# Up-projections of a channel mixer as Strassen block products, with the down-projection interleaved in six parts

## The chip, the core and the metric

The kernel runs on one core of one Trainium2 chip. A core has five engines that work side by side, each through its own instructions in a fixed order: TensorE (PE in the profile, with its weight loads as PEld), VectorE (DVE), ScalarE (ACT), GpSimd (POOL) and SyncE (SP, which here only starts transfers). SBUF is the working memory with 128 partitions, PSUM holds what TensorE accumulates, in eight banks of 512 float32 columns. The metric is the device time of one execution in microseconds.

## The reference

One inference step of two layers over 640 tokens of width 1024: 512 tokens of a new stream, and 16 tokens of each of 8 running streams. Each layer is a mixer followed by a channel mixer on the same residual x. The first mixer is a gated one, the second is attention; neither is changed. The channel mixer is the part that matters:

```python
def _conv_ffn(x, prev, w_up, conv_w, w_down):
    z, st = _causal_dwconv(x @ w_up, conv_w, prev)   # width 3, along the tokens
    gate, up = jnp.split(z, 2, axis=-1)
    return (jax.nn.silu(gate) * up) @ w_down, st
# hp = _rmsnorm(xp, norm_ffn[layer]); D_MODEL = 1024, D_FF = 2816
```

w_up is 1024 x 5632 and w_down is 2816 x 1024. In blocks of 128 features, the up-projection gives 44 blocks (22 of the gate, 22 of the other branch), and the down-projection adds 22 blocks into 8.

## The kernel before

Activations lie with features on partitions and tokens along the free axis. A product keeps float32 accuracy by splitting each operand in two float32r parts, and multiplying three times: high by high, high by low, low by high. So one block of 128 outputs over one chunk of 128 inputs is three passes, each over two halves of 320 tokens: six matmuls of 128x128 weights with 320 moving columns (`mm`, L109). One up-block (8 chunks) is 48 of them.

Each block's weights (128 x 1024 float32) come in by one transfer, issued by SP (`weights`, L87). ScalarE makes the high part (whi, L88), VectorE subtracts for the low part (wlo, L89). Three buffers hold raw, whi and wlo each.

The channel mixer (`ffn`) walks j over 22 pairs of up-blocks: block j of the gate and block 22+j. For each pair TensorE does 96 matmuls. Then, for each of the two blocks, VectorE multiplies the sums by 1/rms of each token (rb) into a padded tile zp (L190, L191), GpSimd puts the running streams' state in (L183) and takes the new state out (L202), ScalarE does the first tap of the convolution (L196) and VectorE the other two (L198). ScalarE applies silu to the gate (L355), VectorE multiplies the two branches (L358, L359), and the product is split again (sh on ScalarE, L97, sl on VectorE, L98). The down-projection comes in four parts of 6, 6, 5 and 5 pairs: after the pairs of a part and one pair ahead, `project` goes through all 8 output blocks, and VectorE adds each into x (L209).

The norm's root is not needed ahead of the products. `prep` makes the operands hh and hl of x times the gain, adds the squares up on GpSimd (acc, L139), and `stats` and `spread` turn the sum into rb: a matmul against ones (L159), a power on GpSimd (L152), five diagonal tiles on VectorE (L170) and a second matmul (L174). The products are under way meanwhile.

The order within each engine is set ahead of time: the program is written in the order of the code, and a scheduling layer moves instructions of an engine past each other by its own estimates of when their inputs will be there. On the chip the engines take their instructions in that order, and wait for each other by semaphores.

## Time and profile before

| | us |
|---|---|
| median of 3 runs (1533.8 to 1535.37) | 1534.4 |
| profiled execution, first to last instruction | 1531.9 |
| PE busy | 1517.8 |
| DVE busy | 899.1 |
| ACT busy | 559.4 |
| POOL busy | 237.4 |
| DVE busy within 228 to 680 us, most of the first channel mixer (452 us) | 262.07 |
| POOL busy within 228 to 680 us | 73.04 |

The profile shows one execution. The share of busy time is taken over all stages together: in the channel mixers (about 215 to 680 us, and 1066 to 1529 us) PE hardly pauses, and DVE is busy somewhat over half of the time. A matmul's own duration (309 ns) is not its cost, since the next one starts before it ends; the cost is the distance between two starts. The median of the runs lies 2.5 us over the profiled span.

### The profile page before, as it was taken

How to read it: one execution, taken by the hardware profiler on the slowest of the kernel's cores; microseconds unless marked ns; L12 is line 12 of the kernel's file. 1: busy time of each engine (PE TensorE's matmuls, PEld its weight loads, DVE VectorE, ACT ScalarE, POOL GpSimd, SP SyncE). 2: the span in 40 equal slices, each digit the busy share in tenths (PEclk: the TensorE clock that was granted, in tenths of full speed). 3: DMA queues.
4: the chain of work that ended last, by engine and by line, in shares of the span. 5: the costliest groups of instructions: out<-in, count | busy, mean ns of one | idle time of the engine just before them, and what ended most of it. 6: DMA issues, size and time to landing. Idle time of an engine off the chain costs nothing.

```text
span 1531.9 us, 26648 instructions
## 1 busy us (share of the span) xinstructions
PE 1517.8 (99%) x11008; PEld 1473.5 (96%) x11008; DVE 899.1 (59%) x1541; ACT 559.4 (37%) x918; POOL 237.4 (15%) x281
## 2 busy tenths in 40 slices
PE   8999999999999999999999999999999999999999
PEld 6999999999999999999989888888999999999998
DVE  6545437644653655675676766768765466365463
ACT  5422334322322322345545454535432233133231
POOL 5000122201210201143111111003221021021010
PEclk9999999999999999999999999999999999999999
DMA  6222212222223222243544343523222222321313
GB/s 226 77 82 73 77 56 85 68 81 85 62 64 95 64 66 93 62 156 103 180 128 136 122 123 104 183 60 107 83 60 76 87 67 57 98 73 53 107 47 106
DMA packets 52296, 142.90 MB, mean 93 GB/s; under 512 B 6656, under 2 KB 13744, under 8 KB 52048
## 3 DMA queue, kind: packets, MB, share of 16 engines
q1 hardware_dynamic: 45424, 133.79, 28.6%
q10 hardware_dynamic: 6752, 7.41, 1.4%
q8 instruction: 87, 1.43, 0.4%
q14 instruction: 33, 0.27, 0.1%
HBM read 125.41 MB, written 11.54 MB: 89 GB/s over the span
## 4 chain that ended last, share of the span: by engine, by line
PE 96%; DVE 2%; issue 1%; ACT 1%; DMA 0%; POOL 0%; SPq 0%; DVEq 0%; ACTq 0%
PE mm L109 71%; PE pj L507 10%; PE pv L583 3%; PE po L109 2%; PE pt L576 1%; PE mm L239 1%; PE pt L662 1%; PE sc L569 1%; DVE hl L132 1%; PE sc L570 1%; DVE wlo L89 1%; PE scs L641 1%; PE pt L537 1%; PE pt L655 0%; PE scs L634 0%
## 5 line engine op out<-in xcount | busy, mean ns | idle before, releaser
L88 ACT CAST whi<-raw 128x1024 fp32r<-128x1024 f32 (+4 forms) x222 | 207.6, 937 | 494.6 <-PE mm L109 426.1
L109 PE MATMUL mm<-hl,whi 128*128 128x320 f32 x1664 | 379.4, 309 | 0.5 <-DVE hl L132 0.5
L109 PE MATMUL mm<-hh,whi 128*128 128x320 f32 x1664 | 379.8, 309 | 0.0
L109 PE MATMUL mm<-hh,wlo 128*128 128x320 f32 x1664 | 379.2, 309 | 0.0
L109 PEld LDWEIGHTS mm<-hl,whi 128*128 128x128 f32 x1664 | 278.2, 188 | 0.7 <-DVE hl L132 0.7
L109 PEld LDWEIGHTS mm<-hh,whi 128*128 128x128 f32 x1664 | 278.2, 188 | 0.1
L109 PEld LDWEIGHTS mm<-hh,wlo 128*128 128x128 f32 x1664 | 278.0, 188 | 0.0
L89 DVE TENSOR_TENSOR wlo<-raw,whi 128x1024 fp32r<-128x1024 f32 (+4 forms) x222 | 245.5, 1107 | 33.3 <-ACT whi L88 33.0
L109 PE MATMUL mm<-sh,wlo 128*128 128x320 f32 x866 | 197.2, 309 | 1.3 <-DVE wlo L89 1.3
L109 PE MATMUL mm<-sl,whi 128*128 128x320 f32 x866 | 197.2, 309 | 0.0
L109 PE MATMUL mm<-sh,whi 128*128 128x320 f32 x866 | 196.2, 309 | 0.0
L202 POOL COPY so<-zp 128x18 f32<-128x18 f32 x88 | 89.4, 1016 | 570.4 <-DVE zp L191 570.4
L190 DVE TENSOR_TENSOR zp<-mm,rb 128x512 f32<-128x512 f32 x88 | 60.9, 692 | 195.8 <-PE mm L109 195.8
L209 DVE TENSOR_TENSOR x<-mm,x 128x640 f32<-128x640 f32 x79 | 65.0, 823 | 185.6 <-PE mm L109 185.6
L198 DVE SCALAR_TENSOR_TENSOR t<-zp,cst,t 128x656 f32<-128x656 f32 x184 | 165.1, 900 | 10.3 <-ACT t L196 5.6
L109 PEld LDWEIGHTS mm<-sh,wlo 128*128 128x128 f32 x866 | 144.6, 188 | 1.6 <-DVE wlo L89 1.6
L109 PEld LDWEIGHTS mm<-sl,whi 128*128 128x128 f32 x866 | 144.8, 188 | 0.0
L109 PEld LDWEIGHTS mm<-sh,whi 128*128 128x128 f32 x866 | 144.4, 188 | 0.2 <-issue 0.2
L507 PE MATMUL pj<-wlo,hh 128*128 128x256 f32 x480 | 137.7, 287 | 0.7 <-DVE wlo L89 0.7
L507 PE MATMUL pj<-whi,hh 128*128 128x256 f32 x480 | 137.7, 287 | 0.0
L507 PE MATMUL pj<-whi,hl 128*128 128x256 f32 x480 | 137.5, 287 | 0.0
L507 PEld LDWEIGHTS pj<-wlo,hh 128*128 128x128 f32 x480 | 91.6, 191 | 2.8 <-issue 1.6
(188 smaller groups left out, 1691.3 us busy)
## 6 DMA issues: line engine op xcount, KB each, us to landing
raw<-w_up SPq DMA_DIRECT2D x88, 512.0 KB
raw<-w_dn SPq DMA_DIRECT2D x32, 384.0 KB
raw<-w_c SPq DMA_DIRECT2D x24, 512.0 KB
raw<-w_dn SPq DMA_DIRECT2D x32, 320.0 KB
raw<-w_ab SPq DMA_DIRECT2D x16, 512.0 KB
ck<-c_k SPq DMA_DIRECT2D x16, 512.0 KB
cv<-c_v SPq DMA_DIRECT2D x16, 512.0 KB
o_kv<-z ACTq DMA_DIRECT2D x8, 640.0 KB
```

The source lines that it names most:

```text
L88: nc.scalar.copy(out=hi[:, c], in_=raw[:, c])
L89: nc.vector.tensor_tensor(out=lo[:, c], in0=raw[:, c], in1=hi[:, c].bitcast(F32), op=ALU.subtract)
L109: nc.tensor.matmul(outs[h], lhsT=l, rhs=r[:, h * HT:(h + 1) * HT], start=start and k == 0, stop=stop and k == 2)
L132: nc.vector.scalar_tensor_tensor(out=lo, in0=x, scalar=gs, in1=hi.bitcast(F32), op0=ALU.mult, op1=ALU.subtract)
L190: nc.vector.tensor_tensor(out=op, in0=a[:, 0:TP], in1=b[:, 0:TP], op=ALU.mult)
L198: nc.vector.scalar_tensor_tensor(out=cv[:, 0:CW], in0=zp[:, i:i + CW], scalar=w[:, i:i + 1], in1=cv[:, 0:CW], op0=ALU.mult, op1=ALU.add)
L202: self.nc.gpsimd.tensor_copy(out=out.rearrange("p (s c) -> p s c", c=2), in_=zp[:, 496:ZW].rearrange("p (s c) -> p s c", c=18)[:, :, 16:18])
L209: self.nc.vector.tensor_tensor(out=x, in0=ps[:, C0:C0 + T], in1=x, op=ALU.add)
L239: nc.tensor.matmul(pvs[tb], lhsT=l[:, tb * P:(tb + 1) * P], rhs=r[:, (kc % 2) * 512:(kc % 2 + 1) * 512], start=kc == 0 and k == 0, stop=kc ...
L507: nc.tensor.matmul(out[tb], lhsT=l[:, tb * P:(tb + 1) * P], rhs=r[:, c:c + 256], start=kc == 0 and i == 0, stop=kc == 7 and i == 2)
L537: nc.tensor.transpose(t[:, tb * P:(tb + 1) * P], z[i][:, tb, pair * P:(pair + 1) * P], k.ident)
L583: nc.tensor.matmul(ov[64 * hh:64 * hh + 64, i * P:n], lhsT=z[2][:, j, (2 * pair + hh) * 64:(2 * pair + hh) * 64 + 64], rhs=u[:, j * P:(j + ...
```

## The change

The two up-blocks of a pair, times the two halves of the input features, times the two halves of the tokens, are a product of 2x2 blocks. It is now worked out with seven block products instead of eight (Strassen's scheme in Winograd's form). Each block product covers 128 outputs, 4 chunks of inputs (512 features: the even chunks or the odd ones) and 320 tokens, so 12 matmuls.

- `forms` replaces `prep` ahead of the channel mixers: for each two chunks of x it makes seven token operands, four of them sums or differences, and splits each in a high and a low part.
- `pair_weights` replaces two calls of `weights`: GpSimd makes four sums and differences of the pair's weights (s1 to s4, 512 columns each, L194 to L198), and ScalarE and VectorE split 3.5 tiles of 1024 columns (A, B, C and half a tile D) instead of 2 (L189, L190).
- `pair_blocks` does the seven products in three PSUM banks X, Z, Y. What is shared between outputs is copied out of a bank by ScalarE while the accumulation goes on (`snap`, four for each pair, L225), and added up on VectorE (L245, L253) and GpSimd (L252).
- `pad_halves` replaces `pad_evac`: three multiplications for each block instead of two (L262). The new state is taken out by ScalarE (L490) instead of GpSimd.
- The down-projection comes in six parts of 4, 4, 4, 4, 3 and 3 pairs, and the blocks of one part are spread among the pairs of the next. The first four pairs have none beside them. The last part follows behind the last pair.
- Pools: three zp tiles instead of four, five temporaries instead of nine in the channel mixers, PSUM as two tiles of two banks and four single banks. The rows of w_up are put into the order of KORD on the way in.

```diff
-PARTS = ((0, 6), (6, 12), (12, 17), (17, 22))
+PARTS = ((0, 4), (4, 8), (8, 12), (12, 16), (16, 19), (19, 22))
+KORD = (0, 2, 4, 6, 1, 3, 5, 7)
...
+    def forms(self, p, x, g, acc, fa, fb):
...
+        def plain(h, l, c, xs, gs):
+            nc.scalar.activation(out=h[:, c], in_=xs, func=AF.Copy, scale=gs)
+            nc.vector.scalar_tensor_tensor(out=l[:, c], in0=xs, scalar=gs, in1=h[:, c].bitcast(F32), op0=ALU.mult, op1=ALU.subtract)
+        plain(ah, al, A, x1[:, A], g1)
+        y1 = self.tmp()[:, 0:T]
+        nc.vector.tensor_scalar(out=y1, in0=x1, scalar1=g1, scalar2=None, op0=ALU.mult)
+        t1 = self.tmp()[:, 0:HT]
+        nc.vector.tensor_tensor(out=t1, in0=y1[:, B], in1=y1[:, A], op=ALU.subtract)
+        nc.scalar.copy(out=bh[:, B], in_=t1)
+        nc.vector.tensor_tensor(out=bl[:, B], in0=t1, in1=bh[:, B].bitcast(F32), op=ALU.subtract)
+        plain(ah, al, B, x2[:, A], g2)
+        plain(bh, bl, A, x2[:, B], g2)
...
+        stt(out=t2, in0=x2[:, B], scalar=g2, in1=t1, op0=ALU.mult, op1=ALU.subtract)
+        stt(out=t3, in0=x2[:, B], scalar=g2, in1=y1[:, B], op0=ALU.mult, op1=ALU.subtract)
+        stt(out=t4, in0=x2[:, A], scalar=g2, in1=t2, op0=ALU.mult, op1=ALU.subtract)
+        nc.scalar.copy(out=ch, in_=t)
+        nc.vector.tensor_tensor(out=cl, in0=t, in1=ch.bitcast(F32), op=ALU.subtract)
...
+    def pair_weights(self, wa, wb):
...
+        A = part(a, 1024, self.wp, w)
+        nc.gpsimd.tensor_tensor(out=s1, in0=b[:, 0:H], in1=b[:, H:2 * H], op=ALU.add)
+        nc.gpsimd.tensor_tensor(out=s2, in0=s1, in1=a[:, 0:H], op=ALU.subtract)
+        B = part(s[0], 1024, self.wp, w)
+        nc.gpsimd.tensor_tensor(out=s3, in0=a[:, 0:H], in1=b[:, 0:H], op=ALU.subtract)
+        nc.gpsimd.tensor_tensor(out=s4, in0=a[:, H:2 * H], in1=s2, op=ALU.subtract)
+        C = part(s[1], 1024, self.wp, w)
+        D = part(b[:, H:2 * H], H, self.fx, ("dhi", "dlo"))
...
+            self.product(X, w["x11"], f, "y1a", True)
+            self.product(Z, w["x12"], f, "y2a", True)
+            p1 = snap(X)
+            self.product(X, w["s2"], f, "t2", False)
+            Y = self.bank()
+            self.product(Y, w["s3"], f, "t3", True)
+        nc.vector.tensor_tensor(out=p1, in0=Z[:, 0:HT], in1=p1, op=ALU.add)
+        u2 = snap(X)
+        self.product(X, w["s1"], f, "t1", False)
+        p7 = snap(Y)
+        self.product(Y, w["x22"], f, "t4", False)
+        v = snap(X)
+        self.product(X, w["s4"], f, "y2b", False)
+        nc.gpsimd.tensor_tensor(out=v, in0=v, in1=p7, op=ALU.add)
+        nc.vector.tensor_tensor(out=u2, in0=Y[:, 0:HT], in1=u2, op=ALU.add)
+        return (p1, X[:, 0:HT]), (u2, v)
...
             for n, (a, b) in enumerate(PARTS):
+                acts, left = [], list(range(8))
                 for j in range(a, b):
-                    if j not in acts:
-                        acts[j] = up(j)
-                if n + 1 < len(PARTS):
-                    acts[b] = up(b)
+                    acts.append(up(j))
+                    if before is not None:
+                        m = -(-len(left) // (b - j))
+                        down(n - 1, before, [(ob,) for ob in left[:m]])
+                        left = left[m:]
+                before = acts
+            down(len(PARTS) - 1, before, [(0, 1)] + [(ob,) for ob in range(2, 8)])
```

How the change moves instructions is seen at three places. Numbers at the end of a name tell tiles apart.

The first place is PE where the first channel mixer begins. Before, the matmuls that turn the norm's sum around (L159, L174) stand among the up-products (mm<-hh, mm<-hl):

```order
L109 MATMUL mm_2009<-hh_1572,whi_2003 128x320 x2
L109 MATMUL mm_2009<-hl_1573,whi_2003 128x320 x2
L109 MATMUL mm_2009<-hh_1572,wlo_2004 128x320 x2
L109 MATMUL mm_2009<-hh_1578,whi_2003 128x320
L159 MATMUL aux_1964<-ones,acc_1571 128x1 x5
L109 MATMUL mm_2009<-hh_1578,whi_2003 128x320
L109 MATMUL mm_2009<-hl_1579,whi_2003 128x320 x2
```

Now (L302 and L317 are the same two steps, sh and sl the last block of the first mixer's projection, fa the new token operands):

```order
L110 MATMUL mm_1964<-sl_1455,whi_1959 128x320 x2
L110 MATMUL mm_1964<-sh_1454,wlo_1960 128x320 x2
L302 MATMUL u_2044<-ones,acc_1477 128x1 x5
L317 MATMUL u_2060<-t_2054,ones 128x128 x4
L317 MATMUL u_2061<-t_2054,ones 128x128
L215 MATMUL u_2102<-fa_1590,whi_2082 128x320
L215 MATMUL u_2102<-fa_1591,whi_2082 128x320
```

Both steps now stand behind the last projection block and ahead of the first up-product, with nothing between them; before, up-products stood ahead of them and between them. At the start of the second channel mixer it is the same.

The second place is DVE in the middle of a channel mixer. Before, one pair:

```order
L190 TENSOR_TENSOR zp_88<-mm_2544,rb_1973 128x512
L191 TENSOR_TENSOR zp_88<-mm_2544,rb_1973 128x8x16
L89 TENSOR_TENSOR wlo_2674<-raw_2672,whi_2673 128x1024
L198 SCALAR_TENSOR_TENSOR t_2646<-zp_88,cst,t_2646 128x656 x2
L190 TENSOR_TENSOR zp_90<-mm_2593,rb_1973 128x512
L191 TENSOR_TENSOR zp_90<-mm_2593,rb_1973 128x8x16
L89 TENSOR_TENSOR wlo_2802<-raw_2800,whi_2801 128x1024
L198 SCALAR_TENSOR_TENSOR t_2655<-zp_90,cst,t_2655 128x656 x2
L358 TENSOR_TENSOR t_2659<-t_2646,t_2655 128x512
L359 TENSOR_TENSOR t_2659<-t_2646,t_2655 128x128
L98 TENSOR_TENSOR sl_2663<-t_2659,sh_2662 128x640
```

Now, half of a pair with its two blocks of the down-projection (L190 are the subtractions for the weights of the next pair, L90 those for the down-projection; L341 are the taps that L198 were, L498 and L499 the product of the branches, L99 is its split):

```order
L190 TENSOR_TENSOR wlo_3337<-s_3323,whi_3336 128x1024
L341 SCALAR_TENSOR_TENSOR t_3243<-zp_89,cst,t_3243 128x656
L245 TENSOR_TENSOR sn_3370<-u_3345,sn_3370 128x320
L90 TENSOR_TENSOR wlo_3470<-raw_3468,whi_3469 128x512
L498 TENSOR_TENSOR t_3247<-t_3233,t_3243 128x512
L499 TENSOR_TENSOR t_3247<-t_3233,t_3243 128x128
L262 TENSOR_TENSOR zp_90<-sn_3370,rb_2053 128x320
L99 TENSOR_TENSOR sl_3251<-t_3247,sh_3250 128x640
L90 TENSOR_TENSOR wlo_3502<-raw_3500,whi_3501 128x512
L253 TENSOR_TENSOR sn_3398<-u_3384,sn_3398 128x320
L190 TENSOR_TENSOR dlo_3555<-raw_3533,dhi_3554 128x512
```

The other half holds five more L262, two additions into x (L352), the subtractions for A and B of the next pair and three more L341: 23 instructions for a pair, where 11 rows with 13 instructions stood before and the down-projection came apart.

The third place is POOL in the same stretch. Before, it moves small columns alone, two of each for a pair (three blocks are shown):

```order
L202 COPY so_1994<-zp_90 128x18
L183 COPY zp_90<-si_1993 128x8x2
L202 COPY so_1994<-zp_89 128x18
L183 COPY zp_89<-si_1993 128x8x2
L202 COPY so_1994<-zp_91 128x18
L183 COPY zp_91<-si_1993 128x8x2
```

Now, one pair:

```order
L194 TENSOR_TENSOR s_3536<-raw_3533 128x512
L197 TENSOR_TENSOR s_3537<-raw_3532,raw_3533 128x512
L252 TENSOR_TENSOR sn_3426<-sn_3426,sn_3412 128x320
L195 TENSOR_TENSOR s_3536<-s_3536,raw_3532 128x512
L198 TENSOR_TENSOR s_3537<-raw_3532,s_3536 128x512
L260 COPY zp_90<-si_2073 128x8x2
L260 COPY zp_88<-si_2073 128x8x2
```

Five additions and subtractions over whole rows of SBUF have come to POOL for each pair, and the copies of the new state have gone from it.

174 lines of the change are left out of this document (131 added, 43 removed).

## The prediction

> **What bounds the kernel now.** I read the busy table and the chain of waits on the page first, then the busy times of the stretch from 228 to 680 us, which is nearly all of the first channel mixer, then the chain in order of time around the places where the two channel mixers begin.
>
> ```profile
> span 1531.9 us, 26648 instructions
> PE 1517.8 (99%) x11008; PEld 1473.5 (96%) x11008; DVE 899.1 (59%) x1541; ACT 559.4 (37%) x918; POOL 237.4 (15%) x281
> PE 96%; DVE 2%; issue 1%; ACT 1%; DMA 0%; POOL 0%; SPq 0%; DVEq 0%; ACTq 0%
> ```
>
> ```profile
> 228.00:680.00 452.00, 452.00 (x3084) 452.00 (x3083) 262.07 (x356) 150.84 (x179) 73.04 (x90) 1.00 0.27 82
> 1043.40:1069.60 26.20, 24.45 (x167) 23.85 (x165) 26.07 (x24) 16.11 (x24) 13.34 (x7) 1.00 0.40 128
> ```
>
> ```profile
> 220.26 1.01 PE aux L159 x10
> 221.27 4.80 PE mm L109 x32
> 226.07 1.11 PE aux L174 x10
> 227.19 452.76 PE mm L109 x3087
> 1063.46 0.81 DVE x L209
> 1066.35 2.90 PE mm L109 x18
> 1069.26 1.01 PE aux L159 x10
> 1070.26 4.80 PE mm L109 x32
> 1075.06 1.11 PE aux L174 x10
> ```
>
> The second fence gives, after the length, the busy times of PE, PEld, DVE, ACT and POOL, then the granted clock. PE is never idle in the channel mixers, and one chain piece of 3087 matmuls lasts 452.76 us: 0.1467 us from one matmul to the next. DVE is busy 58% of that stretch, POOL 16%. There is one other bound: from 1043.4 to 1069.6 us DVE is busy 26.07 of 26.20 us. So fewer matmuls shorten the program as long as DVE, ACT and POOL keep up.
>
> **The matmuls.** A pair takes 84 instead of 96, of the same shape, each with its own weight load as before. 12 x 0.1467 = 1.76 us; 44 pairs give **-77.4 us** (the order has 3696 up-products in place of 4224). The down-projection keeps its count. A middle pair with its two blocks of 24 matmuls now asks for 132 x 0.1467 = 19.36 us, one of the first four pairs of a layer, with nothing beside it, for 12.32. Transfers carry the same bytes.
>
> **VectorE.** Its prices:
>
> ```profile
> L198 DVE SCALAR_TENSOR_TENSOR t<-zp,cst,t 128x656 f32<-128x656 f32 x184 | 165.1, 900 | 10.3 <-ACT t L196 5.6
> L209 DVE TENSOR_TENSOR x<-mm,x 128x640 f32<-128x640 f32 x79 | 65.0, 823 | 185.6 <-PE mm L109 185.6
> L190 DVE TENSOR_TENSOR zp<-mm,rb 128x512 f32<-128x512 f32 x88 | 60.9, 692 | 195.8 <-PE mm L109 195.8
> L191 DVE TENSOR_TENSOR zp<-mm,rb 128x128 f32<-128x128 f32 x88 | 24.8, 282 | 0.0
> L774 DVE TENSOR_TENSOR x<-po,x 128x320 f32<-128x320 f32 x16 | 7.4, 486 | 1.3 <-PE po L109 1.1
> ```
>
> ```profile
> 370.90 0.28 DVE L191 TENSOR_TENSOR zp<-mm,rb 128x128 f32<-128x128 f32 x1
> 371.10 1.22 DVE L89 TENSOR_TENSOR wlo<-raw,whi 128x1024 fp32r<-128x1024 f32 x1
> 372.23 1.83 DVE L198 SCALAR_TENSOR_TENSOR t<-zp,cst,t 128x656 f32<-128x656 f32 x2
> ```
>
> The last two rows show that an instruction starts 0.08 us before the one ahead of it ends, so 1.22 costs 1.14. A middle pair now has 23 of them: three weight subtractions of 1024 columns (3.66), three of 512 (2.07, at the 0.69 of L190), four taps (3.60), the branches' product (0.97) and its split (0.82, as L209), two sums of 320 columns (0.97), six pieces of zp (2.2: two of 320, two of 192 at about 0.35, two of 128), two additions into x (1.65). That is 15.9, less 22 x 0.08: **14.2 us of 19.36**. By itself this fits. A first pair has 11.5 us for 12.32.
>
> **GpSimd's new work on VectorE's port.** What one does to the other shows at the start of the program:
>
> ```profile
> 8.95 14.71 POOL L139 TENSOR_TENSOR acc<-acc,t 128x640 f32<-128x640 f32 x7 [7.88 <-ACT t L138]
> 9.63 5.88 DVE L132 SCALAR_TENSOR_TENSOR hl<-x,gv,hh 128x640 fp32r<-128x640 f32 x3 [0.46 <-ACT hh L131]
> 15.44 2.58 DVE L89 TENSOR_TENSOR wlo<-raw,whi 128x1024 fp32r<-128x1024 f32 x1
> 17.94 4.29 DVE L132 SCALAR_TENSOR_TENSOR hl<-x,gv,hh 128x640 fp32r<-128x640 f32 x2
> 22.15 2.60 DVE L89 TENSOR_TENSOR wlo<-raw,whi 128x1024 fp32r<-128x1024 f32 x1
> 201.01 0.88 DVE L132 SCALAR_TENSOR_TENSOR hl<-x,gv,hh 128x640 fp32r<-128x640 f32 x1
> L139 POOL TENSOR_TENSOR acc<-acc,t x28: 1572/1829/2536, 9.0 to 1066.3; 128x640 f32<-128x640 f32 x28
> ```
>
> While seven additions of 640 columns run on POOL, five subtractions of 0.80 (0.88 alone at 201.01) and two of 1.14 take DVE 15.1 us instead of 6.3. Each addition held DVE up for 8.8 / 7 = 1.25 us; in the busy stretch at 1043 us it is 26.07 against 18.1 us of work, 8.0 / 7 = 1.15. I take 1.2 for 640 columns, in proportion 0.96 for 512 and 0.6 for 320. A pair now brings four of 512, one of 320 and two small copies (0.2 each): **4.8 us** of DVE if all collide with an instruction that reads SBUF twice, nothing if all fall into DVE's pauses.
>
> The Trainium skill ("SBUF — State Buffer", section "Who interferes with whom") has the two engines share one port pair, held by one of them for a whole instruction, and lets a VectorE instruction with one SBUF input pass. By that, POOL's whole 1.57 us would count, 1.26 for 512 columns, and a pair would lose up to 6.2 instead of 4.8. The sum below would be 8 us longer, in the first pairs; the rows show less than that, and I keep them.
>
> **Middle pairs.** 14.2 + 4.8 = 19.0 still fits into 19.36, with nothing to spare. The order decides then. From the end of a pair's first down-block, DVE has an addition into x, the subtractions for A and B, two taps, the second addition into x, a tap and the subtraction for C: 7.6 us, with two collisions 9.5. PE needs C's low part 5.57 us into the next pair, 9.1 us after that same end. So PE waits a few tenths at most pairs. ScalarE's four copies out of PSUM stand behind casts, but have 2 to 3.8 us each before their bank is written again, and ACT has some 10.6 us of work for each pair. Bounds: 0 and 0.75 us a pair; I take 0.25 for the 36 pairs behind the first four of each layer: **+9 us** (0 to 27).
>
> **First four pairs.** 11.5 + 4.8 = 16.3 us of DVE against 12.32 of PE. DVE has a start of about one pair, since the weights of pair 1 are made while PE works at pair 0. Three pairs at 4.0 us less what the start hides (some 2 us): **+10 us a layer, 20 in all** (4 if POOL finds pauses, 34 by all four pairs).
>
> **Where the channel mixers begin.** Before, the two matmuls of the norm (L159, L174) stand among up-products, and PE runs through. Now they stand ahead of the first, so PE waits for the whole way from the last addition into x to rb. Rows for it beyond those above:
>
> ```profile
> L138 ACT ACTIVATE t<-x 128x640 f32<-128x640 f32 x28 | 20.3, 724 | 0.0
> L152 POOL TENSOR_TENSOR rt<-rt,mhalf 128x5 f32<-128x5 f32 x4 | 4.7, 1180 | 7.8 <-DVE rt L151 7.8
> 222.76 1.07 DVE L170 TENSOR_SCALAR t<-cst,rt 128x128 f32<-128x128 f32 x5 [1.29 <-POOL rt L152]
> ```
>
> First mixer: the addition (0.8), five of the forms' instructions of 320 columns (5 x 0.41), a collision with the last acc addition (1.2; the square and that addition run beside it), the split of 960 columns (1.1), then s3 and s4 on POOL with B's subtraction between (3.2), since s3's tile is one that the forms give back, the power (1.2), C's subtraction (1.1), the diagonals (1.1), the second matmul (1.1): 12.9 us. Before, 2.1 us of it were paid (1.01 + 1.11). **+11 us** (8 to 14).
>
> Second mixer: DVE sets the pace already, and forms put in 4.83 us for two chunks (six of 0.41, one over 640 columns 0.47, two of 0.41, one of 960, 1.08) where two of hl took 1.6: 19.3 for 6.4. By DVE's list with its collisions the last addition into x moves from 1063.46 to about 1070.5; behind it stand 7.2 us of forms and two collisions (2.3), then the split, B's subtraction, the diagonals and the second matmul, with hand-overs 15 us: first product at about 1085.5. Before, 87 up-products (55 stand ahead of L159, 32 behind) and the norm's 2.1 us lay within 1076.18, so they would have begun, run together, at 1076.2 - 12.8 = 1063.4. **+22 us** (14 to 30).
>
> **Ends.** The last pair's way from its last product to its split halves is some 7.5 us (pieces 0.6, tap on ACT 0.85, taps 1.6, silu 0.75, product 0.9, splits 1.5, hand-overs and neighbours 1.3); 43 matmuls cover 6.3, where 48 covered 7.0. **+3 us** for both layers (0 to 6).
>
> **Sum**, against the profiled execution: 1531.9 - 77.4 + 9 + 20 + 11 + 22 + 3 = 1519.5; the median of the runs lies 2.5 higher, so 1534.4 - 12.4 = **1522 us**.
>
> **The rivals.**
>
> *GpSimd finds the pauses.* For it: DVE idles some 5 us in a middle pair, and POOL waits too rather than only pushing. Against: at 9 and at 1043 us every addition collided. Terms 0 + 4 + 8 + 14 + 1: -50, about 1484 us.
>
> *VectorE becomes the bound of the middle pairs: slower than before.* Place: its queue, in which instructions that wait (the split for silu's half, the second down-weights, the sum that needs Y, the first addition into x) hold back the subtractions for the next weights. With 19.0 us of work, 1.5 us of pauses that POOL cannot fill make a pair 20.5: 1.1 x 36 = 40 instead of 9, 1553 us. It decides from 0.6 us a pair (12.4 / 36 + 0.25). For it: the sum stands at 98% of the period. Against: each of these waits ends, by my order of events, 1 us or more ahead of what needs it.
>
> *The clock drops in the new pauses.* Granted clock is 1.00 in every stretch shown, but none has PE idle for more than 3 us, and now there are four such pauses. The Trainium skill ("TensorE: Matmul & The Clock Gate", section "What's actually happening") has the clock halve after an idle window of about 3.4 us until as long a busy one; an estimate by it is 1.5 us for each, 6 in all, 1528 us. No row here bears on it.
>
> **Chances.** My sum 0.50, with 1506 to 1537 for itself; pauses found 0.15; VectorE bound 0.26; clock 0.05; gains and losses level 0.04. What can be told from no change is 0.2%, 3 us. Faster 0.64 (most of the sum's case, the first and the third rival), within 0.2% 0.10, slower 0.26. The low end lies near the first rival, the high end past the second: 1490 to 1556.
>
> **What will show it.** 84 up-products a pair, 0.147 us apart; DVE over 90% busy in the first four pairs with PE waiting for wlo of L190; subtractions of 1024 columns at well over 1.24 us on average; PE idle some 11 us ahead of the first product of layer one and DVE the chain from 1043 to about 1085; middle pairs at 19.4 to 19.9 us. I am wrong if middle pairs take over 20 us, or if a matmul into one bank after another does not keep the 0.147.

## The result and the profile after

The change is slower: 1574.7 us (1573.35 to 1577.1, 4 runs) against 1534.9 us of the kernel before beside it, a ratio of 1.0262 with an interval of 1.0247 to 1.0276. The forecast was 1522 us with a range of 1490 to 1556.

The page of the change, its span, the busy table and the chain of waits by engine:

```profile
span 1571.8 us, 26636 instructions
PE 1480.0 (94%) x10480; PEld 1407.0 (90%) x10480; DVE 1199.9 (76%) x1933; ACT 703.6 (45%) x1326; POOL 483.6 (31%) x411
PE 49%; DVE 33%; issue 7%; ACT 4%; DMA 3%; POOL 2%; SPq 0%; ACTq 0%; DVEq 0%; POOLq 0%
```

TensorE has 528 matmuls fewer, and the busy column fell by 38 us. But VectorE's share of the chain went from 2% to 33%: in the channel mixers and on the ways into them TensorE now waits for it.

Where this happens shows in the busy times of stretches (after the length: PE, PEld, DVE, ACT, POOL with their instructions, then the granted clock). The first and third rows are the first four pairs of each layer, the second and fourth the other 18, the last is six pairs in the middle:

```profile
231.13:293.15 62.02, 54.56 (x339) 52.49 (x338) 48.09 (x58) 29.10 (x50) 29.40 (x21) 0.95 0.17 52
293.15:667.85 374.70, 362.15 (x2409) 352.97 (x2408) 316.29 (x426) 169.24 (x293) 145.24 (x124) 1.00 0.25 75
1106.13:1167.27 61.14, 53.98 (x338) 51.92 (x338) 48.52 (x59) 29.65 (x51) 33.93 (x24) 0.95 0.19 61
1167.27:1540.48 373.21, 362.09 (x2409) 352.92 (x2408) 315.81 (x426) 169.17 (x293) 144.95 (x124) 1.00 0.25 76
416.80:537.95 121.15, 119.29 (x795) 116.16 (x793) 106.38 (x139) 55.44 (x97) 47.30 (x42) 1.00 0.26 79
```

A row's length less its matmuls at 0.1467 us is what it lost: 62.02 - 339 x 0.1467 = 12.3 us, 11.6 in the third row; 374.70 - 2409 x 0.1467 = 21.3, and 19.8 in the fourth. A middle pair takes 121.15 / 6 = 20.2 us instead of 19.36. VectorE is busy 106.38 / 6 = 17.7 us of it, so it isn't full. PE's busy column shows less than half of what is lost (121.15 - 119.29 = 1.9 us of 5.0): the distance between starts tells more.

The chain of waits into the first mixer, and into the second:

```profile
215.17 0.83 DVE x L352
220.86 2.18 POOL s L197
223.04 1.23 POOL s L198
226.59 4.05 DVE t L313 x5
230.68 0.80 PE u L317 x2
...
1101.92 2.43 DVE t L313 x2
1104.40 2.08 PE u L317 x8
```

TensorE's last product ahead of the first mixer ends at 215.14, the first of the mixer starts at 231.13: 16.0 us. Less the 2.1 that the norm took before, the step costs 13.9. By the same landmarks (from the end of the attention's last product, at 1039.15 before and 1056.96 now, to the first up-product, which before, with its products run together, would have stood at 1063.4, and now stands at 1106.13) the second costs 49.2 - 24.3 = 24.9 us.

At the end of layer one TensorE waits here (in square brackets the idle time before the row, and what ended it):

```profile
672.61 0.53 PE L110 MATMUL mm<-sh,whi 128*128 128x320 f32 x2 [0.22 <-DVE x L352]
676.37 0.86 PE L110 MATMUL mm<-sh,whi 128*128 128x320 f32 x4 [1.76 <-ACT sh L98]
...
695.65 0.36 PE L654 MATMUL pj<-whi,hh 128*128 128x256 f32 x1 [0.54 <-DVE x L352]
702.11 0.39 PE L654 MATMUL pj<-whi,hl 128*128 128x256 f32 x1 [1.08 <-DVE hl L275]
```

With one more of 0.33 us, and by the distances between starts, that is 5.4 us beyond what the kernel before loses here; the first two and that one come back at the end of layer two, 3.4 us. The whole account:

| term | forecast, us | measured, us |
|---|---|---|
| 528 matmuls fewer | -77.4 | -77.4 |
| way into the first mixer | +11 (8 to 14) | +13.9 |
| way into the second mixer | +22 (14 to 30) | +24.9 |
| first four pairs of both layers | +20 (4 to 34) | +23.9 |
| the other 36 pairs | +9 (0 to 27) | +41.1 |
| ends of the layers | +3 (0 to 6) | +8.8 |
| sum | -12.4 | +35.2 |
| profiled execution | | +39.9 |

Of the 4.7 us that are in no row, 1.8 are lost in the first 23 us of the program: there the granted clock is 0.50 from 19.50 to 22.90 us, where it is 1.00 before, and the same matmul starts 1.8 us later from then on. The rest I can't name. All costs came out above their value, two of them above their range, the middle pairs by far.

### The profile page after: what moved, and what is told of

Same layout as the page of the kernel before. It is cut to its first block, busy times and chain, and to the rows that moved or that the text cites. A ratio compares the mean times of both kernels' runs of the same rounds, so it can differ in the third digit from the quotient of the medians.

```text
span 1571.8 us, 26636 instructions
## 1 busy us (share of the span) xinstructions
PE 1480.0 (94%) x10480; PEld 1407.0 (90%) x10480; DVE 1199.9 (76%) x1933; ACT 703.6 (45%) x1326; POOL 483.6 (31%) x411
## 4 chain that ended last, share of the span: by engine, by line
PE 49%; DVE 33%; issue 7%; ACT 4%; DMA 3%; POOL 2%; SPq 0%; ACTq 0%; DVEq 0%; POOLq 0%
PE mm L110 15%; PE u L215 11%; PE pj L654 10%; DVE t L341 8%; DVE wlo L190 7%; DVE zp L262 7%; DMA raw<-w_up 3%; PE pv L730 3%; PE po L110 2%; DVE x L352 2%; DVE dlo L190 2%; DVE wlo L90 2%; ACT whi L189 2%; PE pt L723 1%; PE mm L382 1%
## 5 line engine op out<-in xcount | busy, mean ns | idle before, releaser
L215 PE MATMUL u<-fa,whi 128*128 128x320 f32 x1408 | 311.4, 311 | 6.8 <-DVE zp L262 4.9
L215 PEld LDWEIGHTS u<-fa,whi 128*128 128x128 f32 x1408 | 236.6, 190 | 8.3 <-issue 3.9
L215 PE MATMUL u<-fa,wlo 128*128 128x320 f32 x704 | 215.0, 315 | 9.0 <-DVE wlo L190 7.7
L90 DVE TENSOR_TENSOR wlo<-raw,whi 128x512 fp32r<-128x512 f32 (+4 forms) x166 | 145.2, 876 | 63.6 <-ACT whi L89 63.4
L89 ACT CAST whi<-raw 128x512 fp32r<-128x512 f32 (+4 forms) x166 | 121.1, 730 | 160.8 <-PE mm L110 86.8
L341 DVE SCALAR_TENSOR_TENSOR t<-zp,cst,t 128x656 f32<-128x656 f32 x184 | 175.2, 980 | 2.9 <-ACT t L339 2.8
L215 PE MATMUL u<-fb,whi 128*128 128x320 f32 x704 | 154.8, 313 | 9.9 <-ACT sn L225 6.6
L262 DVE TENSOR_TENSOR zp<-sn,rb 128x320 f32<-128x320 f32 (+2 forms) x176 | 143.2, 846 | 15.9 <-POOL sn L252 15.6
L215 PEld LDWEIGHTS u<-fa,wlo 128*128 128x128 f32 x704 | 131.8, 190 | 16.7 <-DVE wlo L190 16.7
L215 PEld LDWEIGHTS u<-fb,whi 128*128 128x128 f32 x704 | 117.6, 190 | 12.5 <-ACT sn L225 8.1
L215 PE MATMUL u<-fb,wlo 128*128 128x320 f32 x352 | 112.8, 323 | 12.1 <-DVE wlo L190 11.5
L190 DVE TENSOR_TENSOR wlo<-s,whi 128x1024 fp32r<-128x1024 f32 x88 | 106.8, 1214 | 16.0 <-ACT whi L189 16.0
```

What stands on the lines that cost most here:

```text
L89: nc.scalar.copy(out=hi[:, c], in_=raw[:, c])
L90: nc.vector.tensor_tensor(out=lo[:, c], in0=raw[:, c], in1=hi[:, c].bitcast(F32), op=ALU.subtract)
L190: nc.vector.tensor_tensor(out=l, in0=src, in1=h.bitcast(F32), op=ALU.subtract)
L215: nc.tensor.matmul(out[:, 0:HT], lhsT=l[:, c], rhs=r, start=start and p == 0 and i == 0, stop=p == 3 and i == 2, skip_group_check=True)
L262: m = lambda out, x, y: nc.vector.tensor_tensor(out=out, in0=x, in1=y, op=ALU.mult)
L341: nc.vector.scalar_tensor_tensor(out=cv[:, 0:CW], in0=zp[:, i:i + CW], scalar=w[:, i:i + 1], in1=cv[:, 0:CW], op0=ALU.mult, op1=ALU.add)
```

## The experiments

### What makes a middle pair 20.2 us long

In the rows of the middle the loop can be followed (the expectations count pairs from 0). TensorE waits twice in each pair, for A's low part (by the sixth product of the pair shown, at 417.88, it has lost 0.35 us) and for C's (423.07; 0.45 us with the product behind it): 0.8 us. Between two waits for C's low part lie, among others, in time:

```profile
403.98 0.68 DVE L90 TENSOR_TENSOR wlo<-raw,whi 128x512 fp32r<-128x512 f32 x1
404.69 0.33 SPq L182 DMA_DIRECT2D raw<-w_up  x1
408.28 1.29 POOL L194 TENSOR_TENSOR s<-raw 128x512 f32<-128x512 f32 x1 [4.28 <-DMA raw<-w_up]
409.82 0.49 DVE L253 TENSOR_TENSOR sn<-u,sn 128x320 f32<-128x320 f32 x1 [1.54 <-PE u L215]
410.32 1.04 DVE L190 TENSOR_TENSOR dlo<-raw,dhi 128x512 fp32r<-128x512 f32 x1
411.29 1.17 DVE L262 TENSOR_TENSOR zp<-sn,rb 128x320 f32<-128x320 f32 x1
412.38 2.75 DVE L262 TENSOR_TENSOR zp<-sn,rb 128x192 f32<-128x192 f32 x2
413.69 1.29 POOL L198 TENSOR_TENSOR s<-raw,s 128x512 f32<-128x512 f32 x1
415.52 0.81 DVE L352 TENSOR_TENSOR x<-mm,x 128x640 f32<-128x640 f32 x1
421.80 1.22 DVE L190 TENSOR_TENSOR wlo<-s,whi 128x1024 fp32r<-128x1024 f32 x1
423.07 0.41 PE L215 MATMUL u<-fb,wlo 128*128 128x320 f32 x1 [0.18 <-DVE wlo L190]
```

VectorE waits for D's product (L253, 1.54 us idle). From there to C's low part it has no pause worth naming, 13.2 us. GpSimd's sums begin when b's transfer lands at 408.28 and run to 415, right beside dlo and zp. The chain of waits of this pair goes through these stretched instructions and through no sum:

```profile
409.67 0.63 ACT dhi L189
...
410.32 1.04 DVE dlo L190
411.37 2.15 DVE zp L262 x2
...
413.75 1.39 DVE zp L262
...
416.35 0.98 DVE wlo L190
```

Three explanations were possible: the collisions (theory P), the single tile of D and the order behind it (theory O), and the moment at which b arrives (theory R).

**Without the sums.**

```diff
-        s = [self.fx.tile(...) for _ in range(2)]
+        s = self.fixed        # two tiles, filled once a layer
-        nc.gpsimd.tensor_tensor(out=s1, ...)   # s2, s3, s4 alike
```

> Leaves out GpSimd's four sums and differences of the weights: B and C are split from two tiles that are filled once for each layer, so the output is not the reference's. Everything else, ScalarE's and VectorE's splits and all matmuls included, stays. Theory P (port): these sums run while VectorE makes dlo, zp and wlo, and stretch them; without them zp (L262) falls from 846 ns towards 450, a middle pair from 20.2 to 19.4-19.6 us (36 pairs: -25 us), pairs 2 and 3 of each layer from 16.6-17.5 to 12.5-14 us (-15), and with s3 and s4 gone from the two transitions -3 each: about 1530 us. Theory O (order): the loop from the product of D over its single tile, the state's copy and the cast of A sets the pair, and the sums only fill gaps: middle pairs stay above 20.0 us, and the time is 1555 or more.

Measured: 1504.7 us, 0.9801 (0.9785 to 0.9817) of the kernel before, 70 us below the change, and 25 below what theory P had given.

**The sums on VectorE.**

```diff
-        nc.gpsimd.tensor_tensor(out=s1, in0=b[:, 0:H], in1=b[:, H:2 * H], op=ALU.add)
+        nc.vector.tensor_tensor(out=s1, in0=b[:, 0:H], in1=b[:, H:2 * H], op=ALU.add)
```

with s2, s3 and s4 alike.

> Computes the same as the change, but the four sums of the weights are made on VectorE instead of GpSimd: 4 x 0.69 = 2.8 us more work for VectorE in each pair, and no instruction of 512 columns on GpSimd. Theory P (port): the collisions cost VectorE more than 2.8 us a pair; middle pairs go to 19.4-19.9 us, pairs 2 and 3 of a layer to 14.3-15.5: 1540 to 1555 us. Theory O (order): what counts is the length of VectorE's list between the product of D and the low part of C; it grows by up to 2.8 us: middle pairs 20.5 to 22 us, 1585 to 1620 us.

Measured: 1521.4 us, 0.9911 (0.9896 to 0.9926): 53 us below the change, below the kernel before, and 19 below the low end of theory P. Six middle pairs without the sums, then six with the sums on VectorE:

```profile
392.03:508.11 116.08, 116.08 (x795) 116.08 (x793) 87.83 (x139) 56.89 (x97) 13.84 (x18) 1.00 0.27 83
```

```profile
401.47:517.55 116.08, 116.08 (x794) 116.08 (x793) 104.75 (x163) 57.51 (x97) 13.52 (x18) 1.00 0.27 82
```

Both have 19.35 us a pair. Theory O, which gave a longer pair with the sums on VectorE, is out. Without the sums VectorE is busy 87.83 / 6 = 14.6 us a pair; my forecast of its own work was 14.2. With them on GpSimd 17.7: the collisions take 3.1 us a pair, less than the 4.8 that I had allowed for. So the amount was no reason for 20.2 us, and the run left open what was.

**Two tiles for D.**

```diff
-        D = part(b[:, H:2 * H], H, self.fx, ("dhi", "dlo"))
+        D = part(b[:, H:2 * H], H, self.fx, ("dhi", "dlo"), bufs=2)
```

> Two tiles for dhi and dlo instead of one (and five instead of six snap tiles, for the room). Theory O (order): the cast of D no longer waits for the pair before to finish with it, dlo moves out of VectorE's list behind it, and middle pairs go from 20.2 to 19.4-19.6 us: about 1550 us. Theory P (port): collisions with GpSimd stay as they are, middle pairs 19.9-20.2 us, 1565 to 1575 us.

Measured: 1573.3 us, 1.0252 (1.0236 to 1.0267), no difference from the change. Six middle pairs took 121.43 us. But they are not the same pairs: dlo now starts ahead of D's product, as theory O wanted, and VectorE then waits for v, the last operand of zp:

```profile
431.29 1.63 DVE L262 TENSOR_TENSOR zp<-sn,rb 128x192 f32<-128x192 f32 x2 [2.04 <-POOL sn L252]
```

In the six pairs that is 8.4 us. The wait stands on GpSimd's queue: its addition of v comes behind two or three of the sums, and the first of those waits for b's transfer (it starts as b lands, at 425.91 and 446.12 us in this run). So b's late landing sets a second loop, about as long as the one through D's tile, and two tiles for D alone could show no gain.

**A buffer of its own for b.**

```diff
-        raw = [self.wp.tile([P, 1024], F32, tag="raw", ...) for _ in range(2)]
+        raw = [self.wp.tile([P, 1024], F32, tag="raw", ...), self.fx.tile([P, 1024], F32, tag="rawb", ...)]
```

> The second raw tile of a pair (b) gets a buffer of its own instead of the third place in the ring of three raw tiles that it shares with the down-projection's weights (and five instead of six snap tiles, for the room). Computes the same as the change. Theory R (ring): a middle pair is a loop: b's transfer may start only when VectorE has split the first down-block's weights (404.66 us), lands 3.6 us later (408.3), GpSimd's sums start then and run until 415, beside dlo and zp, A, B and C follow, and behind C the next down-block's split: 20.2 us. With its own buffer b lands up to 13 us earlier, the sums start some 7 us earlier (when a has landed), and middle pairs fall to 19.4-19.6 us; pairs 4 and 5 lose their waits for transfers: 1545 to 1555 us. Theory P (port): the sums take 3 us from VectorE wherever they stand; middle pairs stay at 19.9-20.2 us, 1565 to 1575 us.

Measured: 1549.9 us, 1.0095 (1.0079 to 1.011), 25 us below the change, as theory R had it. Its six middle pairs, the first sum of one of them, and two of VectorE's groups in them:

```profile
414.70:531.89 117.19, 116.64 (x794) 116.12 (x793) 106.67 (x139) 56.90 (x97) 58.25 (x43) 1.00 0.28 82
...
414.60 1.84 POOL L195 TENSOR_TENSOR s<-raw 128x512 f32<-128x512 f32 x1 [6.47 <-DVE wlo L191]
...
L499 DVE TENSOR_TENSOR t<-t,t 128x512 f32<-128x512 f32 x6 | 10.7, 1778 | 0.0
...
L191 DVE TENSOR_TENSOR dlo<-raw,dhi 128x512 fp32r<-128x512 f32 x6 | 4.1, 685 | 0.0
```

The same groups in the change:

```profile
L262 DVE TENSOR_TENSOR zp<-sn,rb 128x128 f32<-128x128 f32 x6 | 8.3, 1376 | 0.0
L190 DVE TENSOR_TENSOR dlo<-raw,dhi 128x512 fp32r<-128x512 f32 x6 | 6.7, 1109 | 0.1
L498 DVE TENSOR_TENSOR t<-t,t 128x512 f32<-128x512 f32 x6 | 4.1, 682 | 0.0
```

VectorE is busy as long as in the change, 106.67 against 106.38 us: the collisions are all still there. But the sums now start at the pair's first product (414.60 and 414.70), as soon as VectorE's subtraction for B has given their tile back, and no longer 11.7 us behind it (408.28 and 396.61 in the change). So they run beside other instructions (the branches' product takes 1778 ns instead of 682, dlo is back at 685), outside the stretch that TensorE waits for. A pair takes 19.5 us. So the late landing of b makes the pair long, and by the chain above it does so through the place of the collisions, not through their amount. The run moves the sums' results forward too, but in the change the chain of the pair holds no sum, and the next run shows that pairs stay long where nothing reads them.

The gain is of the middle alone. The fourth to sixth pair of each layer, which I had expected to win as well, lose 13.6 us against TensorE's pace here and 8.4 in the change.

**Sums that nobody reads.**

```diff
+        t = self.spare        # B and C are split from the fixed tiles
+        nc.gpsimd.tensor_tensor(out=t, in0=b[:, 0:H], in1=b[:, H:2 * H], op=ALU.add)   # and three more
```

> As in the run without sums, B and C are split from two tiles filled once (the output is not the reference's), but GpSimd still does the four sums of each pair, from the raw tiles, into a spare tile that nobody reads. So the collisions stay and nothing waits for the sums, except that raw tile a is held until they are done. Theory P (port): as the change in the middle, 19.9-20.2 us a pair, first four pairs 16-17 us: 1555 to 1570 us. Theory R (ring, with A, B and C waiting for the sums): middle pairs 19.4-19.5 us in spite of some 3 us of collisions in each: 1515 to 1530 us.

Measured: 1581.4 us, 1.0295 (1.028 to 1.0311), a little slower even than the change and above both expectations; a middle pair takes 122.01 / 6 = 20.3 us. The run was meant to free VectorE from waiting for the sums, and didn't: GpSimd's addition of v (the last operand of zp) stands behind the first sum, and that waits for b's transfer.

```profile
L268 DVE TENSOR_TENSOR zp<-sn,rb 128x192 f32<-128x192 f32 x6 | 8.6, 1434 | 13.5 <-POOL sn L258 13.5
```

VectorE idles 13.5 / 6 = 2.25 us a pair ahead of zp. Instructions without a reader still stand in a queue. So this run doesn't tell the collisions from the wait for v, but it shows again that b's landing holds the pair, here with no reader of the sums.

**Both together: sums on VectorE, and the buffer for b.** The two diffs above in one.

> The sums on VectorE and the own buffer for b together. Computes the same. With the sums on VectorE the middle pairs were already at 19.4 us, and some 7 us a layer were lost in pairs 4 and 5. Theory V (VectorE's backlog: 11.5 + 2.8 = 14.3 us of work in each of the first four pairs against 12.3 of TensorE, 2 us a pair, paid at pairs 4 and 5): the buffer changes nothing, 1518 to 1524 us. Theory R (transfers come late there too): 7 us a layer less, 1506 to 1512 us.

Measured: 1518.7 us, 0.9899 (0.9885 to 0.9914). The interval overlaps with that of the sums on VectorE alone: no difference that these runs can tell, as theory V had it. Six middle pairs for the four cases:

| | raw tiles shared | own tile for b |
|---|---|---|
| sums on GpSimd | 121.15 us | 117.19 us |
| sums on VectorE | 116.08 us | 116.16 us |

Either remedy alone takes nearly all of the middle pairs' wait away. Of the 53 us between sums on GpSimd and sums on VectorE, some 27 lie in the 36 later pairs, 22 in the first four of both layers, and 5 on the ways into the mixers.

### What the interleaving does by itself

**Seven products with the down-projection in four parts, as before.**

```diff
-PARTS = ((0, 4), (4, 8), (8, 12), (12, 16), (16, 19), (19, 22))
+PARTS = ((0, 6), (6, 12), (12, 17), (17, 22))
...
+                done[b] = up(b)
+                down(n, [done[j] for j in range(a, b)], ...)
```

> The seven-product pairs with the down-projection as before: four parts of 6, 6, 5 and 5 pairs, each part's eight blocks in one piece behind its pairs and one more. Computes the same. If VectorE needs 16 to 17.5 us a pair while TensorE needs 12.3, then what holds the change back is relieved by the interleaving alone: without it some 16 pairs of each layer lose 4 to 5 us, where now 4 lose 3 and 18 lose 1.1: 1630 to 1690 us. If VectorE can make up in the down-projections (8 x 36 matmuls, 42 us) what it lost: 1580 to 1610 us.

Measured: 1618.1 us, 1.0544 (1.052 to 1.0567): 43 us more than the change. That lies between the two expectations. While a part's eight blocks run, VectorE works ahead: the first pair behind them loses nothing, the second 1.3 us, the third already 5 to 7.

**The kernel before with six interleaved parts.**

```diff
-PARTS = ((0, 6), (6, 12), (12, 17), (17, 22))
+PARTS = ((0, 4), (4, 8), (8, 12), (12, 16), (16, 19), (19, 22))
...
+                    acts.append(up(j))
+                    if before is not None:
+                        down(n - 1, before, ...)
```

> The kernel before with nothing but the down-projection in six interleaved parts: plain up-blocks of 48 matmuls. Computes the same. VectorE is at 58% there, so I expect no wait from the interleaving: 1530 to 1538 us. If the interleaved order itself costs something (VectorE's additions into x ahead of what the next pair needs, a raw tile held by the down-weights), it shows here: 1540 us or more.

Measured: 1540.1 us, 1.0036 (1.0023 to 1.005). The interleaving alone costs some 5 us, and the trace shows where:

```profile
686.74 0.55 PE L512 MATMUL pj<-whi,hh 128*128 128x256 f32 x1 [4.71 <-DVE x L209]
```

The last part now has three pairs, so a block of it is 18 matmuls, 2.64 us. VectorE has an addition into x (0.81), a split (0.55) and hl (0.87) for each, and meets GpSimd's addition of the squares, beside which an hl took up to 2.21: it can't follow, and the attention's first product waits 4.7 us. Behind the pause the granted clock is 0.50 up to 691.54, which costs another 2 us; the profiled execution was the longest of the five. This wait doesn't come from the seven products. I put it down to the size of the last part; no run changes that size alone. The change waits at the same place, by the 0.54 and 1.08 us in the rows of its ends.

### The ways into the mixers

**The norm's products behind the first up-products.**

```diff
-        k.aux = k.bank
+        k.aux = lambda: k.psum()[:, 0:512]
```

> The norm's two products take their PSUM from the two-bank tiles, which are free in the first four pairs, instead of the four single banks X, Z and Y come from; the order then has 26 of the first pair's products ahead of the first norm product. Theory N (the norm stands in the way): PE's pause of 16 us ahead of the first mixer falls under 4 us and the one ahead of the second by as much, the clock stays at 1.00 at the first: -10 to -12 us in layer one, -8 to -20 in layer two: 1543 to 1557 us. Rival (VectorE is the bound there): the pause only moves behind the first products, the second and third pair wait longer by what the first gained, since VectorE's forms, splits and diagonals are the same: 1566 us or more.

Measured: 1563.4 us, 1.0186 (1.0171 to 1.0202), 11 us less than the change. The first up-product of layer one starts at 213.28 instead of 231.13, that of layer two some 30 us earlier by the same landmark, but more than half of it is given back within the first pair, which waits for forms, splits and diagonals. A new pause of 7.0 us ahead of the attention, whose norm takes its PSUM from the two-bank tiles as well, costs some more. The truth lies between the two: the norm stood in the way, and VectorE's list right behind it.

**The same on the kernel with VectorE's sums and the own buffer.**

```diff
-        k.aux = k.bank
+        k.aux = lambda: k.psum()[:, 0:512]
...
     rt, rb = both(acc)
+    k.aux = k.bank
```

> The kernel of the run above, and the norm's two products ahead of the channel mixers in the two-bank tiles (the norm behind the first mixer keeps its bank). Computes the same. Theory N (norm in the way): some 11 us less than the run above, as the same step gave on the change; the clock stays at 1.00 at the start of the first mixer: 1507 to 1513 us. Theory V: what the first pair gains is lost in the pairs behind it, since VectorE's list is the same; less than 5 us.

Measured: 1512.9 us, 0.986 (0.9845 to 0.9875), 5.8 us less than the run it builds on: between theory V (less than 5) and N (some 11), nearer to V.

**The squares summed by TensorE, and one product of the forms on ScalarE.**

```diff
-            nc.gpsimd.tensor_tensor(out=acc, in0=acc, in1=sq[:, :T], op=ALU.add)
+        for tb in range(5):
+            nc.tensor.matmul(self.ssum[:, tb:tb + 1], lhsT=sq[:, tb * P:(tb + 1) * P], rhs=self.ones[:, 0:1],
+                             start=c == 0, stop=c == 7, skip_group_check=True)
...
-        nc.vector.tensor_scalar(out=y1, in0=x1, scalar1=g1, scalar2=None, op0=ALU.mult)
+        nc.scalar.activation(out=y1, in_=x1, func=AF.Copy, scale=g1)
```

> The kernel of the run above, and in the forms: the squares of each chunk are summed by TensorE straight into one PSUM bank (five products of one column a chunk) instead of by GpSimd's additions of 640 columns, and the product of x and the gain (0.47 us, four a layer) goes from VectorE to ScalarE. Computes the same. Theory P/V (collisions with those additions at 1.2 us each and VectorE's list set the way into the second mixer): eight collisions, 9.6, and four x 0.4 = 11 us less there, some 3 less at the first: 1493 to 1500 us. If TensorE's or ScalarE's hand-overs set it: less than 4 us.

Measured: 1505.8 us, 0.9813 (0.9798 to 0.9827), 7.1 us less, between the two expectations. In this run and the next, the sums of the prompt's tokens lack the squares of the first chunk, by the start flags; no instruction is missing.

**A first part of three pairs.**

```diff
-PARTS = ((0, 4), (4, 8), (8, 12), (12, 16), (16, 19), (19, 22))
+PARTS = ((0, 3), (3, 7), (7, 11), (11, 15), (15, 19), (19, 22))
```

> The kernel of the run above with parts of 3, 4, 4, 4, 4 and 3 pairs: three pairs instead of four have no down-projection beside them. Computes the same. Theory V (2 us of backlog for VectorE in each pair without down-blocks): 2 us a layer less, 4 in all. If pairs 4 and 5 lose their time to transfers: no change within 1 us.

Measured: 1502.5 us, 0.9789 (0.9773 to 0.9805), 3.4 us less, as theory V had it.

**The sums of squares whole.**

```diff
-                             start=c == 0, stop=c == 7, skip_group_check=True)
+                             start=c == 0 and tb == 0, stop=c == 7, skip_group_check=True)
```

> The kernel of the last run with one flag changed. In the two runs ahead of this one each of the five columns of the bank in which TensorE sums the squares was opened by a start flag of its own, and the sums of the prompt's four columns (not of the last, the streams') come out without the first chunk's squares. Here only the first column's first product carries the flag. If a start flag throws away the state of the whole bank, so that the next product into a neighbouring column replaces instead of adding, all sums are whole now. Computes what the change computes. The time is that of the last run, 1500 to 1505 us, since no instruction is added or moved.

Measured: 1500.0 us, 0.9777 (0.9762 to 0.9791). The sums are whole with this one flag. This is the fastest version: 34 us below the kernel before, 75 below the change. Its 18 later pairs of layer two:

```profile
1120.89:1469.11 348.22, 348.02 (x2371) 347.39 (x2370) 304.56 (x485) 172.04 (x289) 46.30 (x53) 1.00 0.27 80
```

TensorE is busy 348.02 of 348.22 us and loses under 1 us against its pace, with VectorE at 304.56, 87% of the stretch, where it was 85% in the change. In layer one the same pairs lose 3.6 us, all of it in the first of them.

**TensorE's sums of squares on the change alone.**

```diff
-            nc.gpsimd.tensor_tensor(out=acc, in0=acc, in1=sq[:, :T], op=ALU.add)
+            nc.tensor.matmul(self.ssum[:, tb:tb + 1], ..., start=c == 0 and tb == 0, stop=c == 7, ...)
```

> The change with one step alone: TensorE sums the squares ahead of the channel mixers (with the one start flag) instead of GpSimd's additions of 640 columns. Computes the same. Theory P (port): eight additions that meet VectorE's forms cost 1.15 to 1.25 us each on the way into the second mixer, two or three of them count at the first: 1560 to 1566 us. If VectorE's own list or ScalarE's casts set that way (as the pair without sums suggests, where the way into the second mixer was 3.3 us shorter, not more): 1568 to 1574 us.

Measured: 1572.4 us, 1.026 (1.0241 to 1.0278): no difference from the change that these runs can tell. The way into the second mixer is 2.4 us shorter in the profiled execution. GpSimd's additions on VectorE's port, which I had priced at eight times 1.2 us, were not what set that way. The chain of that run, just ahead of the first product:

```profile
1090.16 1.16 DVE fb L159
...
1091.46 2.18 POOL s L198
1093.64 1.23 POOL s L199
...
1095.97 1.22 DVE wlo L191
1097.19 3.89 DVE t L314 x4
...
1101.13 1.22 PE u L318 x4
```

Behind the last of the forms the third and fourth sum, the cast and split of C, and the diagonals follow one after the other: 11 us without any addition of squares. The power for the root stands behind both sums on GpSimd, the diagonals behind C's split on VectorE, and the norm's second product ahead of the first up-product.

## Why the prediction was wrong

**The matmuls** held: 0.147 us from one to the next also where they change banks, -77.4 us.

**VectorE's work** held: 14.2 us a pair forecast, 14.6 measured. **GpSimd's collisions** were oversized in sum (4.8 forecast, 3.1 measured) and undersized each: I took 0.96 for a sum of 512 columns by proportion, and a zp piece of 128 columns went from 0.28 to 1.38 us, +1.1. The Trainium skill's page "SBUF — State Buffer", section "Who interferes with whom", has the port locked for the whole instruction; by that a sum of 1.29 us costs up to that much, and the row agrees better with it than my proportion. All together the stretching comes to some three such: dlo gets 0.4 us longer and two zp pieces of 320 columns 0.3 each on the mean, two other pieces 1.1 each. I had also not followed the Trainium skill's lock to its end: by the 6.2 us a pair that I worked out from it, a middle pair would ask VectorE for 14.2 + 6.2 = 20.4 us, more than the 19.36 of TensorE, so the middle pairs too would have become longer, and not only the first.

**Middle pairs** is the step that failed, by 32 us of the 53 between forecast and measurement: +9 forecast, 0.25 us a pair, and +41.1 measured, 0.8 us in a regular pair and 1.14 on the mean. It said: "The order decides then. From the end of a pair's first down-block, DVE has an addition into x, the subtractions for A and B, two taps, ...: 7.6 us, with two collisions 9.5", against 9.1 that TensorE gives. The list doesn't begin there. The last matmul of the first down-block starts at 413.14, but VectorE comes to that addition only at 415.52, straight from dlo and zp, and those can't begin ahead of D's product, at 409.8. I had spread the collisions over the pair and put two of them into the stretch behind the down-block; all 3.1 us fall into the part ahead of it, because b's transfer lands there, and b waits for the ring of three raw tiles, a resource that I hadn't followed at all.

That the list's number nearly held is luck. From 415.52 to C's low part at 423.02 VectorE takes 7.5 us with no collision, so C's low part comes 9.7 us after the down-block's last product, beside my 9.5: a start 2.2 us late stands in for two collisions that weren't there. Even the 9.5 would have made 0.4 us a pair, and I took 0.25. Nor had I A's low part, for which TensorE waits as well. The rest of the 41.1 us is in irregular pairs: the sixth of each layer loses 2.7 and 2.4 us, with a wait for a raw tile's transfer in the chain, and the last five up to 2.1.

**The rival that came nearest** was the second, VectorE in the middle pairs, with 0.26. Its bound for deciding, 0.6 us a pair, was passed, at 0.8 to 1.2. Its mechanism was half right: a queue in which instructions that wait hold back the next weights, yes; a VectorE without room, no, since the same busy time fits into 19.5 us where the sums stand elsewhere. Its 40 us for these pairs were nearly the 41.1 measured, by another mechanism; its 1553 us were too low, since the other terms came out above their value too.

**First four pairs**: +20 forecast, +23.9 measured, inside its range. VectorE is the bound there: the fourth pair of each layer takes 17.4 us by the distance of first products, VectorE is busy 16.5 of them in layer one, and my sum was 16.3. (The upper end of 34 should have been 32: eight pairs at 4.0.)

**The ways into the mixers**: +11 and +22 forecast, +13.9 and +24.9 measured, inside their ranges. What is missing in both is mostly one row: the five diagonals (L313) were priced at 1.1 us by the row of before and took 4.05 and 3.1, beside sums on GpSimd. One of them takes up to 1.30 us in the change, and at most 0.56 with the sums on VectorE. That the second came out inside its range is in part luck: taking GpSimd's additions of squares away, whose collisions I had counted there, made the way 2.4 us shorter and the program no faster that these runs can tell.

**Ends**: +3 forecast, +8.8 measured. I had the last pair's way to its split, and that wait is 2.3 us in each layer, 4.6 instead of 3. I hadn't the waits for additions into x (2.1 in both layers), nor the attention's first products, which wait for x and hl (2.1) behind a last part with blocks of 18 matmuls.

**The clock**, the third rival, came true beside the rest. Windows around the first product of layer one:

```profile
220.00:225.00 5.00, 1.71 (x9) 1.62 (x8) 1.99 (x3) 0.71 (x1) 4.14 (x3) 0.50 0.16 34
231.00:233.00 2.00, 2.00 (x9) 2.00 (x9) 0.00 (x0) 0.27 (x1) 0.90 (x1) 0.50 0.03 8
235.00:238.00 3.00, 3.00 (x22) 3.00 (x21) 0.13 (x1) 0.45 (x2) 0.00 (x0) 1.00 0.00 0
```

The granted clock is 0.50 in the pause and for 3.4 us of work behind it, in which matmuls stand 0.267 us apart: 1.6 us there and 1.1 at layer two, inside the terms of the first four pairs. The Trainium skill's page "TensorE: Matmul & The Clock Gate", section "What's actually happening", gives about 3.4 us for the window of both, and this trace agrees at this place. The estimate of 1.5 for a pause was right; at the two ends no pause was long enough. It is 0.50 once more in the fourth pair of each layer (285.74 to 289.15 and 1159.55 to 1162.96), where TensorE waits for VectorE; what that adds isn't told apart here.

## What to carry to other kernels

A sum of work that fits into the period doesn't settle it: follow the loop from one wait of the bound engine to the next through every queue, and ask where in it the new instructions fall, which is set by when their input arrives, here by a ring of buffers. When a remedy changes nothing, look whether a second loop of the same length has taken over, as with the two tiles for D. A helper engine that shares a port is nearly free only outside that loop: here the same four additions cost 53 us more on GpSimd than on the engine that they were to relieve. And when a change moves an engine from 58% to nine tenths, price the short stretches too: starts, ends and parts with no cover made 71.5 of the 112.6 us of costs.

## What the runs showed of the hardware

- **A collision can last nearly as long as GpSimd's instruction, and works both ways.** VectorE's instruction of 128, 192 or 512 columns with two SBUF operands gets up to 1.1 us longer beside a sum of 1.29 us, whatever its own length (0.28 to 1.38, 0.36 to 1.45, 0.68 to 1.78 us). With the own buffer, where the sums met longer instructions, they took longer themselves: 1.84 us for the first, in its row above, instead of 1.29.

- **An instruction with one SBUF operand is stretched too.** The five diagonals (a tile times a scalar) took 4.05 us beside GpSimd's sums, and 1.07 in the kernel before without them. The Trainium skill, "SBUF — State Buffer", section "Who interferes with whom", names this kind among those that can take both ports, and lets an instruction with one SBUF input pass only where it does not; the row agrees.
- **The way back to the full clock can be longer than 3.4 us.** In the run with the norm in the two-bank tiles, TensorE paused 7.0 us ahead of the attention and then worked at half the clock for over 7 us:

```profile
680.00:687.00 7.00, 0.29 (x2) 0.02 (x1) 5.86 (x5) 2.58 (x4) 3.71 (x2) 0.81 0.50 165
687.00:694.50 7.50, 7.20 (x33) 7.21 (x34) 2.33 (x9) 0.00 (x0) 3.84 (x10) 0.50 0.11 41
```

  In the kernel before with six parts it was 4.8 us, behind a pause of 4.7. Why longer than at 231 us isn't settled; the work there is of another shape (10 products of one column, then 256 columns; in the other kernel 256 at once).
- **A start flag works on a whole PSUM bank.** With a flag for each of five columns in one bank, only the column opened last (the streams') kept the first chunk: the prompt's output came out some 13% off, the streams' whole. With one flag on the first column all five were whole. The Trainium skill's page "PSUM — Partial Sum Buffer", section "The four PSUM rules", states that the flag clears the written marks of the whole bank, not of the columns that it writes; the two runs agree.
